# A mixture-of-experts decoder trunk on one core: VectorE's part of the overflow block's search ahead of the branch, and the down product's column halves as two tiles

## Chip, cores and metric

One core of a Trainium2 chip runs the whole program. The metric is the device time of one execution in microseconds; times are medians of several runs. Where an expert gets more tokens than its fixed slots hold, the program branches into a further block; the inputs are the same in every run.

## What is computed

Two layers on 512 tokens of 1024 columns, fp32. Each layer is a token mixer (layer 0: causal differential attention; layer 1: causal pooling over trailing windows), a layer norm, a mixture of experts, and a layer norm. The mixers are not touched by the change. The experts' part of the reference, cut down (a router picks one of 4 groups for each token and the two best of the group's 8 experts):

```python
def hier_moe(x, ..., w_gate, w_up, w_down):
    g_idx = argmax(xf @ w_grp_router + b_grp_router)            # group of a token
    top_v, top_i = top_k(expert logits in that group, 2)
    gate = g_p * softmax(top_v)
    ...                                                         # tokens sorted by expert
    def run_block(xb, e):
        h = silu(xb @ w_gate[e]) * (xb @ w_up[e])               # 1024 -> 512
        return h @ w_down[e]                                    # 512 -> 1024
    out[token] += gate * run_block(...)
h = layer_norm(alpha * h + hier_moe(h))
```

## The kernel before

All 32 experts of a layer run, two at a time (a pair, 16 pairs in a layer), each with 64 slots for tokens, so that a pair fills the 128 partitions. An expert that gets more than 64 tokens has the rest done in an overflow block behind a branch. On these inputs one overflow block runs in layer 0 and none in layer 1.

Weights come over the SyncE queue in loads of 1 MB into 21 buffers (`fill` issues as buffers come free, `take` hands them out in order). A pair takes 12 of them: 4 for gate, 4 for up, 4 for down.

`moe` (L890) holds a layer's experts. Its loop (q from 0 to 7) does an even and an odd pair:

- `gather2` (L1030, with `gather`, L905): VectorE writes a one-hot matrix G (token by slot, in `place_in`, L576 to L580, one buffer), TensorE multiplies tokens by it in four rounds of 32 matmuls (L917), and ScalarE and VectorE take each round out of PSUM to xT (L901, L903).
- `gate_of` (L1206, with `gate_up`, L961): 32 gate matmuls into psg, 32 up matmuls into psu (L969); ScalarE makes sg = silu(psg) (L976), VectorE h = sg * psu (L978).
- `flip`: four transposes of h on TensorE (L983), copied out by ScalarE (hT, L984).
- `down` (L986): 32 matmuls (L994) into y, one PSUM tile of two banks, a bank for each half of the 1024 columns. `weigh` (L1001) multiplies by the slots' weights and splits the result in a high and a low part, in a tile yy: ScalarE reads y for the high part (L1003), VectorE for the low (L1004), for each half.
- `spread_all` (L1192, with `spread_sum`, L1197): for each of four token tiles TensorE brings the yy of the two pairs before back to token rows (sc, L1201 and L1202, a PSUM tile with two buffers), and VectorE adds it to the running sum r (L1204). Column half 0 is done after an even pair's `gate_of`, half 1 after its `flip`.

The last round of the loop ends otherwise. After the odd pair's `gate_of` the engines load the number of overflow blocks and branch (L1260, L1264). Inside, SyncE fetches gate and up weights of the two experts, and `seek` (L1131) finds the block's tokens: VectorE marks the experts (hit), sums their weights (msk, wc), computes slot numbers (base, then sl, shown as msk) and what is left (rem), then writes G for the block; TensorE gathers (64 matmuls of L917), and `places` makes the way back. After the branch stand `spread_all` of half 0, `flip`, `spread_all` of half 1, and `down_spread` (L1015), which does the down product one column half after the other and puts the way back of half 0 (L1008, L1009, r in L1011) between the steps of half 1. A second branch (L1294) holds the block's gate and up product, a third (L1300) its `item_down`, again with `down_spread`. So `down_spread` runs three times: in layer 0, for the block, and in layer 1. Between the branches, `after()` of layer 0 converts the first weights of layer 1's mixer (pc: ScalarE L283, VectorE L284), and the layer ends with a norm.

TensorE's order is the order in which the program is written (`manual_schedule`, L1130). VectorE's and ScalarE's order is chosen by a scheduler, which keeps to the dependencies between tiles: a read and a write of one tile are kept in order even where they touch different halves of it.

Of the kernel before, what the change touches and what calls it, by code (L numbers as in the profile page):

```python
# [8 lines left out]
F32 = mybir.dt.float32  # L9
F32R = mybir.dt.float32r  # L10
# [54 lines left out]
def tile_trunk(ctx, tc, x, w_qkv, w_o, p_in, p_grp, p_scale, p_out,  # L65
# [180 lines left out]
    def do(steps):  # L246
        for f in steps:
            f()
# [641 lines left out]
    def moe(l, rt_in, name1, after):  # L890
        with ExitStack() as es:
# [10 lines left out]
                else:  # L902
                    V.tensor_scalar(dst, src, g, b, op0=OP.mult, op1=OP.add)  # L903

            def gather(slots, cc, xT, pairs):  # L905

                n = pairs * P
                G = keep.tile([P, NT, 2 * P], F32R, name="G", tag="G")
                for j in range(NT):
                    do(place_in(G[:, j, 0:n], slots, cc, j))  # L910

                def round(k0, ga):
                    for k in range(k0, k0 + 2):
                        for j in range(NT):
                            g = G[:, j] if pairs == 2 else G[:, j:j + 1, 0:P].to_broadcast([P, 2, P])
                            for i in range(2):
                                PE.matmul(ga[:, k - k0], half_of(xs[j], i).bitcast(F32R)[:, k], g,  # L917
                                          start=j + i == 0, stop=j + i == NT)
                    for k in range(k0, k0 + 2):
                        factor(xT[:, k, 0:n], ga[:, k - k0, 0:n], k, (ACT, V)[k % 2])  # L920

                def ga_tile(k0):
                    if k0 in (2, 4):
                        return p2.tile([P, 2, 2 * P], F32, name="ga", tag="sc")
                    return p1.tile([P, 2, 2 * P], F32, name="ga", tag="ga")

                return G, [lambda k0=k0: round(k0, ga_tile(k0)) for k0 in range(0, KD, 2)]

            def flip_places(G, i, Sm, ga):

# [55 lines left out]
            def down(hT, wd, wslot, todo=()):  # L986

                todo = list(todo)
                y = p1.tile([P, 2, 512], F32, name="y", tag="y")
                for k in range(4):  # L990
                    for c in range(2):
                        for e in range(2):
                            es_ = slice(e * CAP, (e + 1) * CAP)
                            PE.matmul(y[es_, c], hT[:, k, es_], wd(e, k, c), start=k == 0, stop=k == 3)  # L994
                    run(todo)
                yy = unit("yy")
                for c in range(2):
                    weigh(yy, y, wslot, c)
                return r32(yy)

            def weigh(yy, y, wslot, c):  # L1001
                yr = r32(yy)
                ACT.activation(yr[:, c], y[:, c], AF.Copy, scale=wslot)  # L1003
                V.scalar_tensor_tensor(yr[:, 2 + c], y[:, c], wslot, yy[:, c], op0=OP.mult, op1=OP.subtract)  # L1004

            def spread(yr, Sm, t, c, st=None):
                ps = p2.tile([P, 512], F32, name="sc", tag="sc")
# [6 lines left out]

            def down_spread(hT, wd, wslot, Sm, yy, st):  # L1015

                y = p1.tile([P, 2, 512], F32, name="y", tag="y")
                for c in range(2):
                    for k in range(4):
                        for e in range(2):  # L1020
                            es_ = slice(e * CAP, (e + 1) * CAP)
                            PE.matmul(y[es_, c], hT[:, k, es_], wd[c][e][:, k], start=k == 0, stop=k == 3)
                        if c and k < 2:
                            for t in (2 * k, 2 * k + 1):
                                spread(r32(yy), Sm, t, 0, st)
                    weigh(yy, y, wslot, c)
                for t in range(NT):
                    spread(r32(yy), Sm, t, 1, st)
# [99 lines left out]
            rt_in.region.close()  # L1128
            fill(CAP0)
            es.enter_context(tc.manual_schedule(engines={mybir.EngineType.PE}))  # L1130
            def seek(xT1, Sm1):  # L1131

                hit, left = rt([2, NE], "hit"), rt([2], "left")
                for e in range(2):
                    V.tensor_scalar(hit[:, e], cf[:, C_I32:C_I32 + NE], ixf[:, e:e + 1], None, op0=OP.is_equal)
                wc, wx = rt([2, NT], "wc"), rt([NT, 4], "wx", F32R)
                wt = wtmp
                for e in range(2):
                    V.tensor_tensor(wt, wsum, hit[:, e:e + 1].to_broadcast([P, NT, NE]), op=OP.mult)
                    V.tensor_reduce(wc[:, e], wt, axis=AX, op=OP.add)  # L1140
                split(wx[:, :, 0:2], wx[:, :, 2:4], wc[:, :, :].rearrange("p e t -> p t e"))

                base, sl = rt([2], "base"), wtmp.rearrange("p t e -> p (t e)")
                V.tensor_scalar(base, m8[:, 0:2], 0.5, 1e6, op0=OP.is_lt, op1=OP.mult)
                V.scalar_tensor_tensor(base, m8[:, 0:2], float(CAP), base, op0=OP.mult, op1=OP.add)
                V.scalar_tensor_tensor(base, ixf, float(S), base, op0=OP.mult, op1=OP.add)
                for e in range(2):
                    V.tensor_scalar(sl[:, e * CAP:(e + 1) * CAP], slotc[:, 0:CAP], base[:, e:e + 1], None, op0=OP.add)
                V.tensor_tensor(rem, rem, hit[:, 0], op=OP.subtract)
                V.tensor_tensor(rem, rem, hit[:, 1], op=OP.subtract)  # L1150
                V.tensor_scalar(rem, rem, 0.0, None, op0=OP.max)
                G1, rounds = gather(sl, code, xT1, 1)
                do(rounds)
                places(G1, wx, Sm1, ws1)

# [68 lines left out]
            for q in range(NPAIR // 2):  # L1224
                p, final = 2 * q, q == NPAIR // 2 - 1

                fill(CAPW)
                if final:
                    gb, rows_ = norm_rows(l, 1, lambda: p2.tile([P, 512], F32, name="row", tag="sc"))
                else:  # L1230
                    rows_ = [lambda i=i: residue(i) for i in (0, 2, 1, 3)]
                prev = [(yr, places_of(b)) for yr, b in prev]
                h = gate_of(p, rows_[0:2] if final else rows_[2:4] if q == 1 else ())
                if q == 0:
                    R = two("r")
                    whole(0)
                    whole(1)
                wdn = [take("d", l, p, i) for i in range(2)]
                fill(CAPW)
                if prev:  # L1240
                    spread_all(0, prev)
                else:
                    code_row(0)
                    code_row(1)
                hT = hT_tile()
                flip(h, hT)
                if prev:
                    spread_all(1, prev)
                else:
                    all_weights()  # L1250
                prev = [down_of(p, hT, wdn)]

                p += 1
                fill(5 if final else CAPW)
                h = gate_of(p, rows_[2:4] if final else rows_[0:2] if q == 0 else ())
                wdn = [take("d", l, p, i) for i in range(2)]
                if final:
                    prev = [(yr, places_of(b)) for yr, b in prev]
                    Sm, ws = places_of(p), wall[:, p:p + 1]
                    n_items = nc.values_load(items[0:1, 0:1], min_val=0, max_val=2 * MAXB)  # L1260
                    wx = [[two("wx") for _ in range(2)] for _ in range(2)]
                    xT1 = mo.tile([P, KD, 2 * P], F32, name="xT1", tag="xT")[:, :, 0:P]
                    Sm1 = mo.tile([P, S], F32R, name="Sm1", tag="Sm", bufs=3)
                    with tc.If(n_items, preferred_fallthrough_block=False):  # L1264
                        er = experts()
                        fetch(w_gate, er, wx[0])
                        fetch(w_up, er, wx[1])
                        seek(xT1, Sm1)
                    spread_all(0, prev)
                    hT = hT_tile()  # L1270
                    flip(h, hT)
                    spread_all(1, prev)
                    yy = unit("yy")
                    down_spread(hT, wdn, ws, Sm, yy, st)
                    done(4)
                else:
                    fill(CAPW)
                    xT, (G, rounds) = gather2(p + 1)
                    do(rounds[0:2])
                    hT = hT_tile()  # L1280
                    flip(h, hT)
                    do(rounds[2:4])
                    prev.append(down_of(p, hT, wdn))
# [111 lines left out]
```

## Time and profile before

| | |
|---|---|
| three runs | 1479.14, 1480.89, 1483.9 us; median 1480.89 |
| profiled execution | 1484.56 us |
| its span on the core | 1482.8 us |
| mean granted TensorE clock | 0.982 of full speed |
| busy: TensorE, VectorE, ScalarE | 96%, 44%, 23% of the span |
| DMA | 450.16 MB, mean 304 GB/s |

The span runs from the first to the last instruction; the execution's own time holds 1.76 us more. Layer 0's experts take roughly from 300 to 840 us of the span, layer 1's from 990 on. In the timeline a row gives the start and the length of one instruction or of several alike in a row, and in brackets how long the engine had been idle before it and what ended that.

### The profile page before, as it was taken

What the parts mean: (1) busy time and instruction counts of PE and PEld (TensorE: products, weight loads), DVE (VectorE), ACT (ScalarE), POOL (GpSimd) and SP (SyncE); (2) the same over time, 40 slices, a digit from 0 to 9 for tenths busy, and PEclk for the clock granted to TensorE, in tenths of its full rate; (3) what the DMA queues carried; (4) which work ended last, traced back from release to release, by engine and by line L of the source; (5) the groups of instructions that cost most, each with busy time, mean ns of one, the idle gap of its engine ahead of it and who ended that gap; (6) DMA issues with size and microseconds to landing.
All of it is one profiled execution on the core that took longest, in us unless ns stands there. A gap on an engine that the chain in (4) does not pass through costs nothing. (4 is left out here: it accounts for less than half of the span.)

```text
span 1482.8 us, 18487 instructions
## 1 busy us (share of the span) xinstructions
PE 1416.7 (96%) x7269; PEld 806.0 (54%) x7269; DVE 654.5 (44%) x1513; ACT 345.6 (23%) x714; POOL 26.9 (2%) x24
## 2 busy tenths in 40 slices
PE   8999999999999999999988699999999999999993
PEld 6766776855455445444543387864445444544541
DVE  4356358575423223313224697466423312322136
ACT  4355456421111011011111144331011011110110
POOL 0000000210000000000000000110000000000000
PEclk9999999999999999999999899999999999999997
DMA  7111505379999999999994315379999999999971
GB/s 255 59 53 33 187 13 194 128 306 392 414 417 421 421 421 421 421 421 421 421 411 164 131 57 235 115 286 389 396 422 420 422 421 420 421 421 420 422 290 58
DMA packets 85712, 450.16 MB, mean 304 GB/s; under 512 B 10664, under 2 KB 20464, under 8 KB 36464
## 3 DMA queue, kind: packets, MB, share of 16 engines
q1 hardware_dynamic: 85616, 448.86, 75.2%
q8 instruction: 62, 1.02, 0.3%
q14 instruction: 34, 0.28, 0.1%
HBM read 446.74 MB, written 2.10 MB: 303 GB/s over the span
## 5 line engine op out<-in xcount | busy, mean ns | idle before, releaser
L969 PE MATMUL psu<-w_u,xT 128*64 128x512 f32 x1024 | 225.6, 593 | 0.0
L969 PE MATMUL psg<-w_g,xT 128*64 128x512 f32 x1024 | 225.3, 593 | 0.2 <-ACT xT L901 0.2
L994 PE MATMUL y<-w_d,hT 128*64 128x512 f32 x960 | 212.6, 596 | 1.5 <-ACT hT L984 1.5
L1004 DVE SCALAR_TENSOR_TENSOR yy<-y,wall,yy 128x512 fp32r<-128x512 f32 x64 | 47.2, 738 | 330.6 <-ACT yy L1003 329.1
L969 PEld LDWEIGHTS psg<-w_g,xT 128*64 128x64 f32 x1024 | 73.4, 137 | 145.6 <-issue 141.8
L969 PEld LDWEIGHTS psu<-w_u,xT 128*64 128x64 f32 x1024 | 72.8, 137 | 142.6 <-issue 137.6
L994 PEld LDWEIGHTS y<-w_d,hT 128*64 128x64 f32 x960 | 66.3, 137 | 128.5 <-issue 123.0
L976 ACT ACTIVATE sg<-psg 128x512 f32<-128x512 f32 x33 | 19.7, 597 | 467.2 <-PE psg L969 467.1
L917 PE MATMUL ga<-G,xs 128*128 128x256 f32 x960 | 121.5, 285 | 4.3 <-DVE G L579 4.3
L917 PEld LDWEIGHTS ga<-G,xs 128*128 128x128 f32 x960 | 115.8, 191 | 16.8 <-issue 11.4
L1201 PE MATMUL sc<-yy,Sm 128*128 128x512 f32 x240 | 101.9, 424 | 6.5 <-DVE r L1204 5.2
L978 DVE TENSOR_TENSOR h<-sg,psu 128x512 f32<-128x512 f32 x33 | 35.6, 1078 | 159.2 <-PE psu L969 159.2
L1204 DVE TENSOR_TENSOR r<-r,sc 128x512 f32<-128x512 f32 x128 | 85.8, 684 | 33.4 <-PE sc L1202 33.3
L1202 PE MATMUL sc<-yy,Sm 128*128 128x512 f32 x240 | 94.8, 395 | 0.0
L291 PE MATMUL acc<-pc,xTh 128*128 128x512 f32 x192 | 77.6, 404 | 2.4 <-ACT pc L256 2.1
L292 PE MATMUL acc<-pc,xTh 128*128 128x512 f32 x192 | 77.2, 402 | 0.8 <-DVE pc L257 0.8
L293 PE MATMUL acc<-pc,xTl 128*128 128x512 f32 x192 | 77.5, 404 | 0.0
L1201 PEld LDWEIGHTS sc<-yy,Sm 128*128 128x128 f32 x240 | 45.1, 188 | 41.6 <-DVE r L1204 21.2
L901 ACT ACTIVATE xT<-ga,gcol 128x256 f32<-128x256 f32 (+1 forms) x60 | 33.5, 558 | 144.6 <-PE ga L917 144.6
L903 DVE TENSOR_SCALAR xT<-ga,gcol 128x256 f32<-128x256 f32 (+1 forms) x60 | 32.1, 534 | 68.8 <-ACT xT L901 68.8
L1003 ACT ACTIVATE yy<-y,wall 128x512 fp32r<-128x512 f32 x64 | 43.8, 684 | 59.4 <-DVE yy L1004 41.3
L984 ACT ACTIVATE hT<-tp 128x512 f32<-128x512 f32 x33 | 19.7, 598 | 147.7 <-PE tp L983 146.2
(314 smaller groups left out, 1796.3 us busy)
## 6 DMA issues: line engine op xcount, KB each, us to landing
w_g<-in_moe_w_gate_dram SPq DMA_DIRECT2D x128, 1024.0 KB
w_u<-in_moe_w_up_dram SPq DMA_DIRECT2D x128, 1024.0 KB
w_d<-in_moe_w_down_dram SPq DMA_DIRECT2D x128, 1024.0 KB
w_a<-in_attn_w_qkv_dram SPq DMA_DIRECT2D x16, 512.0 KB
x<-in_x_dram SPq DMA_DIRECT2D x8, 512.0 KB
w_v<-in_attn_w_qkv_dram SPq DMA_DIRECT2D x4, 1024.0 KB
w_wo<-in_attn_w_o_dram SPq DMA_DIRECT2D x4, 1024.0 KB
wx<-in_moe_w_gate_dram SPq DMA_DIRECT2D x4, 1024.0 KB
```

The lines of the kernel that those rows point to most:

```text
L291: PE.matmul(acc, xhl(0, k), wh, start=start and j == 0, stop=False)
L292: PE.matmul(acc, xhl(0, k), wl, start=False, stop=False)
L293: PE.matmul(acc, xhl(1, k), wh, start=False, stop=stop and j == len(order) - 1)
L917: PE.matmul(ga[:, k - k0], half_of(xs[j], i).bitcast(F32R)[:, k], g, start=j + i == 0, stop=j + i == NT)
L969: PE.matmul(ps[es_], xT[:, k, es_], ws2[e][k // 4][:, k % 4], start=k == 0, stop=k == KD - 1)
L978: V.tensor_tensor(h[:, :, :].rearrange("s k q -> s q k"), r(sg), r(gu[1]), op=OP.mult)
L994: PE.matmul(y[es_, c], hT[:, k, es_], wd(e, k, c), start=k == 0, stop=k == 3)
L1003: ACT.activation(yr[:, c], y[:, c], AF.Copy, scale=wslot)
L1004: V.scalar_tensor_tensor(yr[:, 2 + c], y[:, c], wslot, yy[:, c], op0=OP.mult, op1=OP.subtract)
L1201: PE.matmul(ps, sm, yr[:, c], start=i == 0, stop=False)
L1202: PE.matmul(ps, sm, yr[:, 2 + c], start=False, stop=i == len(ys) - 1)
L1204: V.tensor_tensor(r, r, ps, op=OP.add)
```

## The change

1. `seek` is cut in two. `aim` has VectorE's search and the writing of G for the overflow block (and the split of wc on ScalarE and VectorE); `seek` keeps the gather and the way back. In the last round `aim` is called ahead of the odd pair's `gate_of`, outside of the branch, so it runs in both layers. `gather` takes a G that is there already.
2. The PSUM tile y of two banks becomes two tiles of one bank each, y0 and y1, in `down`, `down_spread` and `weigh`.

```diff
-            def gather(slots, cc, xT, pairs):
+            def gather(slots, cc, xT, pairs, G=None):
...
-                G = keep.tile([P, NT, 2 * P], F32R, name="G", tag="G")
-                for j in range(NT):
-                    do(place_in(G[:, j, 0:n], slots, cc, j))
+                if G is None:
+                    G = slot_places(slots, cc, n)
...
+            def slot_places(slots, cc, n):
+                G = keep.tile([P, NT, 2 * P], F32R, name="G", tag="G")
+                for j in range(NT):
+                    do(place_in(G[:, j, 0:n], slots, cc, j))
+                return G
...
-                y = p1.tile([P, 2, 512], F32, name="y", tag="y")
+                y = [p1.tile([P, 512], F32, name=f"y{c}", tag=f"y{c}") for c in range(2)]
...
-                            PE.matmul(y[es_, c], hT[:, k, es_], wd(e, k, c), start=k == 0, stop=k == 3)
+                            PE.matmul(y[c][es_], hT[:, k, es_], wd(e, k, c), start=k == 0, stop=k == 3)
...
-                ACT.activation(yr[:, c], y[:, c], AF.Copy, scale=wslot)
-                V.scalar_tensor_tensor(yr[:, 2 + c], y[:, c], wslot, yy[:, c], op0=OP.mult, op1=OP.subtract)
+                ACT.activation(yr[:, c], y[c], AF.Copy, scale=wslot)
+                V.scalar_tensor_tensor(yr[:, 2 + c], y[c], wslot, yy[:, c], op0=OP.mult, op1=OP.subtract)
...
-            def seek(xT1, Sm1):
+            def aim():
 
                 hit, left = rt([2, NE], "hit"), rt([2], "left")
...
-                G1, rounds = gather(sl, code, xT1, 1)
+                return slot_places(sl, code, P), wx
+
+            def seek(xT1, Sm1, found=None):
+
+                G1, wx = found or aim()
+                G1, rounds = gather(None, None, xT1, 1, G1)
                 do(rounds)
                 places(G1, wx, Sm1, ws1)
...
+                if final:
+                    found = aim()
                 p += 1
                 fill(5 if final else CAPW)
                 h = gate_of(p, rows_[2:4] if final else rows_[0:2] if q == 0 else ())
...
-                        seek(xT1, Sm1)
+                        seek(xT1, Sm1, found)
```

The scheduler moves more than these lines show. TensorE's and SyncE's order stay as they were. VectorE's order at the branch, before (h of the last pair, then the branch and the search in it; `msk` with `base` is sl):

```order
L978 TENSOR_TENSOR h<-sg,psu 128x128x4
L1260 TENSOR_LOAD items
L1264 COMPARE_AND_BRANCH
L1264 UNCONDITIONAL_BRANCH
L1135 TENSOR_SCALAR hit<-cf,ixf 128x32 x2
L1139 TENSOR_TENSOR msk<-ph,hit 128x128
...
L1148 TENSOR_SCALAR msk<-cf,base 128x64 x2
L578 TENSOR_SCALAR G<-msk,code 128x128 x2
L579 SCALAR_TENSOR_TENSOR G<-msk,code,G 128x128 x2
```

And now:

```order
L983 TENSOR_TENSOR h<-sg,psu 128x128x4
L1272 TENSOR_LOAD items
L1276 COMPARE_AND_BRANCH
L1276 UNCONDITIONAL_BRANCH
L903 TENSOR_SCALAR xT_5635<-ga,gcol 128x128 x4
L948 COPY pwc<-pw 128x4
L952 TENSOR_TENSOR ws_3038<-pwc 64x1 x2
```

Inside the branch only the copies out of the gather and the slots' weights are left. The sixteen operations of the search stand now at the head of the layer, after `pick` and before the first h of the layer, in both layers; the eight writes of G stand among the copies (L903) of the last gather of the loop.

VectorE's order around h of an even pair in the middle of a layer, before (yy of the pair before, r of the sums):

```order
L1004 SCALAR_TENSOR_TENSOR yy_4363<-y_4346,wall_3010,yy_4363 128x512
L978 TENSOR_TENSOR h_4384<-sg_4419,psu_4402 128x128x4
L1004 SCALAR_TENSOR_TENSOR yy_4363<-y_4346,wall_3010,yy_4363 128x512
L1204 TENSOR_TENSOR r0_3101<-r0_3101,sc_4438 128x512
L1204 TENSOR_TENSOR r0_3101<-r0_3101,sc_4444 128x512
```

And now:

```order
L1009 SCALAR_TENSOR_TENSOR yy_4371<-y0_4353,wall_3010,yy_4371 128x512
L1009 SCALAR_TENSOR_TENSOR yy_4371<-y1_4354,wall_3010,yy_4371 128x512
L983 TENSOR_TENSOR h_4392<-sg_4427,psu_4410 128x128x4
L1214 TENSOR_TENSOR r0_3101<-r0_3101,sc_4446 128x512
L1214 TENSOR_TENSOR r0_3101<-r0_3101,sc_4452 128x512
```

The second yy has moved ahead of h, in all pairs but the first two and the last, where it stood there already. ScalarE's order is the same there (sg, yy, yy), but its second yy no longer waits for VectorE's first.

TensorE's order in `down_spread`, layer 0, before, at the change from half 0 to half 1 (sc: the sums of half 0; in brackets the engines and queues that a matmul waits for):

```order
L1022 MATMUL y_5790<-w_d_0_15_0_1_5427,hT_5766 64x512
L1022 MATMUL y_5790<-w_d_0_15_1_0_5556,hT_5766 64x512 [waits DMAHW3_49,DVE_49]
L1022 MATMUL y_5790<-w_d_0_15_1_1_5558,hT_5766 64x512 [waits DMAHW4_49]
L1008 MATMUL sc_5803<-yy_5789,Sm_5564 128x512 [waits Activation_49]
L1009 MATMUL sc_5803<-yy_5789,Sm_5564 128x512
```

And now:

```order
L1027 MATMUL y0_5805<-w_d_0_15_0_1_5441,hT_5781 64x512
L1027 MATMUL y1_5806<-w_d_0_15_1_0_5601,hT_5781 64x512 [waits DMAHW3_49]
L1027 MATMUL y1_5806<-w_d_0_15_1_1_5603,hT_5781 64x512 [waits DMAHW4_49]
L1013 MATMUL sc_5819<-yy_5804,Sm_5609 128x512 [waits DVE_49,Activation_49]
L1014 MATMUL sc_5819<-yy_5804,Sm_5609 128x512 [waits DVE_49]
```

The wait for VectorE has left the first matmul of half 1 and stands at the sums. At the end of layer 0 two conversions move besides: on ScalarE the half 1 yy of `down_spread` now comes ahead of one pc that it came after, and VectorE's closing norm has two pc (L284) between its steps, where it had one.

## Rows read from the trace of the kernel before

**Rows 1.** The page, busy time by engine.

```profile
PE 1416.7 (96%) x7269; PEld 806.0 (54%) x7269; DVE 654.5 (44%) x1513; ACT 345.6 (23%) x714; POOL 26.9 (2%) x24
```

**Rows 2.** Windows: length, busy time by engine, granted clock, DMA share, GB/s.

```profile
600.00:660.00 60.00, 59.70 (x308) 28.16 (x305) 17.44 (x32) 7.11 (x12) 0.00 (x0) 1.00 1.01 421
...
772.00:774.00 2.00, 2.00 (x11) 2.00 (x11) 0.00 (x0) 0.00 (x0) 0.00 (x0) 0.50 1.05 434
1434.00:1436.00 2.00, 2.00 (x12) 0.66 (x10) 0.67 (x1) 0.00 (x0) 0.00 (x0) 1.00 0.54 203
```

**Rows 3.** Timeline of SyncE, two issues of the weight queue, 24 loads apart.

```profile
631.75 1.58 SPq L147 DMA_DIRECT2D w_g<-in_moe_w_gate_dram  x2
...
690.14 0.80 SPq L147 DMA_DIRECT2D w_g<-in_moe_w_gate_dram  x2
```

**Rows 4.** TensorE's waits, whole run: us in total, times, longest.

```profile
PE sc L1201 <- DVE r L1204: 5.2, 18, 0.3
PE y L1022 <- DVE yy L1004: 4.7, 3, 1.6
```

**Rows 5.** Timeline at the branch of layer 0.

```profile
766.60 1.03 DVE L978 TENSOR_TENSOR h<-sg,psu 128x512 f32<-128x512 f32 x1 [5.09 <-PE psu L969]
767.65 0.39 DVE L1135 TENSOR_SCALAR hit<-cf,ixf 128x32 f32<-128x32 f32 x2
...
769.81 0.48 DVE L578 TENSOR_SCALAR G<-msk,code 128x128 fp32r<-128x128 f32 x2
...
770.61 0.76 PE L917 MATMUL ga<-G,xs 128*128 128x256 f32 x4 [4.08 <-DVE G L579]
...
771.61 8.82 PE L917 MATMUL ga<-G,xs 128*128 128x256 f32 x60 [0.23 <-DVE G L579]
```

**Rows 6.** Source line L1264, TensorE's branch: durations, first and last start.

```profile
L1264 PEldq COMPARE_BRANCH  x3: 75/240/307, 762.9 to 1440.1; - x3
```

**Rows 7.** Timeline, two rounds of an ordinary gather.

```profile
645.39 4.01 PE L917 MATMUL ga<-G,xs 128*128 128x256 f32 x32
```

**Rows 8.** Timeline of VectorE, the first h of layer 0.

```profile
324.57 1.04 DVE L978 TENSOR_TENSOR h<-sg,psu 128x512 f32<-128x512 f32 x1 [2.60 <-PE psu L969]
```

**Rows 9.** Timeline, the last `down_spread`, from half 0 to half 1.

```profile
1451.99 1.08 PE L1022 MATMUL y<-w_d,hT 128*64 128x512 f32 x4 [1.57 <-DVE yy L1004]
...
1453.33 0.40 PE L1009 MATMUL sc<-yy,Sm 128*128 128x512 f32 x1
```

**Rows 10.** Timeline, the first sum of half 1: layer 0, layer 1.

```profile
800.92 0.50 PE L1008 MATMUL sc<-yy,Sm 128*128 128x512 f32 x1 [1.38 <-ACT yy L1003]
...
1458.99 0.50 PE L1008 MATMUL sc<-yy,Sm 128*128 128x512 f32 x1 [0.79 <-ACTq L1294]
```

**Rows 11.** Timeline, sums of half 0 in the middle of layer 0.

```profile
674.40 1.08 DVE L978 TENSOR_TENSOR h<-sg,psu 128x512 f32<-128x512 f32 x1 [4.86 <-PE psu L969]
...
675.33 0.72 DVE L1004 SCALAR_TENSOR_TENSOR yy<-y,wall,yy 128x512 fp32r<-128x512 f32 x1
...
675.97 1.27 DVE L1204 TENSOR_TENSOR r<-r,sc 128x512 f32<-128x512 f32 x2
...
675.99 0.40 PE L1202 MATMUL sc<-yy,Sm 128*128 128x512 f32 x1
...
676.69 0.51 PE L1201 MATMUL sc<-yy,Sm 128*128 128x512 f32 x1 [0.30 <-DVE r L1204]
```

**Rows 12.** Timeline of VectorE, closing norm of layer 0.

```profile
843.41 0.70 DVE L284 SCALAR_TENSOR_TENSOR pc<-w_pin,vcol,pc 128x512 fp32r<-128x512 f32 x1
```

**Rows 13.** Timeline of TensorE, the last up product of layer 1.

```profile
1433.51 6.18 PE L969 MATMUL psu<-w_u,xT 128*64 128x512 f32 x28
```

**Rows 14.** Timeline, start of layer 1's mixer: two readers of PSUM beside TensorE.

```profile
847.56 3.86 PE L263 MATMUL pp<-cf,r 128*128 128x128 f32 x17 [8.09 <-DVE r L407]
...
849.50 1.36 DVE L257 TENSOR_TENSOR xTl<-pp,xTh 128x512 fp32r<-128x512 f32 x2
849.53 0.60 ACT L256 ACTIVATE xTh<-pp 128x512 fp32r<-128x512 f32 x1 [0.20 <-PE pp L263]
```

More of the change, by code (lines that the diff above doesn't have):

```diff
@@ L1015, in down_spread @@
             def down_spread(hT, wd, wslot, Sm, yy, st):
-                y = p1.tile([P, 2, 512], F32, name="y", tag="y")
+                y = [p1.tile([P, 512], F32, name=f"y{c}", tag=f"y{c}") for c in range(2)]
                 for c in range(2):
@@ L1021, in down_spread @@
                             es_ = slice(e * CAP, (e + 1) * CAP)
-                            PE.matmul(y[es_, c], hT[:, k, es_], wd[c][e][:, k], start=k == 0, stop=k == 3)
+                            PE.matmul(y[c][es_], hT[:, k, es_], wd[c][e][:, k], start=k == 0, stop=k == 3)
                         if c and k < 2:
```

## The prediction, made before the changed kernel was run

> **What bounds the kernel now.** I read the page first: TensorE is busy for 96% of the span [rows 1]. So the time is TensorE's own work plus its waits, and a change of VectorE's work counts only where TensorE waits for VectorE. In the middle of a layer the windows show a granted clock of 1.00 and a DMA share of 1.01 at 421 GB/s [rows 2]: TensorE runs with almost no gap, and the weight stream is as full as it gets. Two issues of the weight queue, 24 loads of 1.0486 MB apart, lie 58.39 us apart [rows 3], so TensorE takes 25.17 MB in 58.39 us, or 431 GB/s, a little more than the stream's 421. It lives off the 21 buffers that were filled ahead. Next I read TensorE's waits [rows 4], and for each group that the change touches the timeline around one of its waits.
>
> The sum is made against the profiled execution (1484.56 us), 3.67 above the median of the runs (1480.89). I take the gain as the same in both. A difference of some 4.4 us, 0.3%, is what a measurement of this kernel can tell from none.
>
> **1. The search ahead of the branch (layer 0 alone runs the block).** Before, VectorE ends h at 767.63, begins the search 0.02 us later, begins the first G at 769.81, and TensorE starts to gather at 770.61 after 4.08 us of idle time, with 0.23 more before the other 60 matmuls [rows 5]. With G written before, those 4.08 + 0.23 = 4.31 us go. TensorE's own branch stood at 762.9 [rows 6], 3.6 us before its last matmul ended (770.61 - 4.08 = 766.53), so I take the entry of the block as hidden. The gather itself took from 770.61 to 780.43, 9.82 us less 0.23 of wait, and the granted clock was 0.50 in 772 to 774 [rows 2, 5], the 1.2 GHz level of the two, after the idle time. The same 64 matmuls at full clock take two rounds of 4.01 us, 8.02 [rows 7]. In the new order TensorE comes into the gather straight from the dense up product, so I take the full clock: 1.57 us more. Together **5.9 us**. Lower bound 4.3, if the clock falls anyway. The block's fetch of expert weights stays on its queue as it is, and TensorE uses them only behind the next pair's down product and sums, so it doesn't hold the gather.
>
> What that search costs in its new place: the order puts it before the layer's first h, where VectorE was idle for 2.60 us [rows 8]. It lasted 769.81 - 767.65 = 2.16 us [rows 5]; so it fits, with 0.44 left for the small split of weights (wx) that moves along, at a price of **0**. If the cover were gone, 2.16 us in both layers would delay h, less what TensorE does there ahead of needing h (the code rows). The eight G's follow the last gather of the loop, while TensorE has a down product and a gate and up product before the next h: 0 as well. In layer 1 the search and the G's are made for nothing, at the same places.
>
> **2. Column halves in three down_spreads.** Before, the first matmul of half 1 waits until VectorE has read half 0 out of the two-bank tile: 4.7 us in 3 waits [rows 4], 1.57 in the last layer [rows 9]. In the new order that matmul waits for the weights alone. What is late next is the sum behind it: its second matmul needs VectorE's yy, which is ready at 1451.99 (TensorE's release). Four half-1 matmuls take 1.0 us and fit into the 1.57. So the second matmul of the sum moves from 1453.33 [rows 9] to 1451.99, 1.34 us earlier. Three times: **4.0 us**. The upper bound is the whole 4.7; the lower 2.8, if VectorE's read runs 0.4 later because ScalarE's next read goes beside it.
>
> **3. Half 1 in layer 0.** TensorE waited 1.38 us for ScalarE's yy, because a pc conversion stood ahead of it there; in layer 1, with nothing ahead, it was 0.79 [rows 10]. ScalarE now does yy first: **0.6 us**, between 0 and 0.6.
>
> **4. The sums in the loop.** Before, VectorE did yy, h, yy, and then the r additions; ScalarE's second yy waited for VectorE's first, and VectorE's second came after h. So r stood 0.65 us behind h (675.97 against 675.33), and TensorE, which has two PSUM buffers for the sums, waited for r [rows 11]. In the cadence of the matmuls the next would have started at 675.99 + 0.23 = 676.22; it started at 676.69: 0.47 us. Now both yy stand ahead of h (both halves of y have been finished since before the gate product), and r comes 0.65 earlier than it did, ahead of 676.22. The waits count 18 such stops, 5.2 us in all [rows 4]: one for each of the 14 even pairs that have sums between gate and flip (7 in a layer), shown as 0.30, and four in the closing pairs, where both yy stood ahead of h already. I take 0.45 for each of the 14, nearest the cadence: **6.3 us**; bounds 14 x 0.30 = 4.2 and 14 x 0.47 = 6.6.
>
> **5. What gets worse.** In layer 0's closing norm one more pc conversion of VectorE now lies between its steps. One that is there already takes 0.70 us and stands among the statistics [rows 12]. TensorE waits for the end of that chain, so the second one costs **0.7 us**; 0 at best.
>
> Sum: 5.9 + 4.0 + 0.6 + 6.3 - 0.7 = 16.1. From 1480.9 that is **1464.8 us** (1468.5 against the profiled one).
>
> **Rivals.**
> *The block's entry takes the place of the wait.* If TensorE needs until 770.6 to have the instructions of the block, 7.7 us after its branch at 762.9 [rows 6], part 1 gives nothing and the time is 1470.7. The old trace cannot exclude it, since the wait for G covers it. Against it: VectorE took the same branch and began its search 0.02 us after h [rows 5]. The Trainium skill ("Runtime: NRT & Kernel Launch", Instruction fetch mechanics) speaks for it: a taken branch to a target outside of the prefetched window makes the engine fetch by DMA before it goes on. It gives no time for that; VectorE's row shows no stall that h did not cover. Chance 0.06.
>
> *The stream becomes the bound.* At 421 GB/s [rows 2] two pairs need 25.17 / 0.421 = 59.8 us, against 58.39 of TensorE's [rows 3]; with part 4 it would be 57.9. So each two pairs eat 1.9 us of lead rather than 1.4. At the end of layer 1 the stream falls off in 1434 to 1436 [rows 2]; the last four loads are down weights, 2.5 us each at 421, so the up weights were there by about 1425. The up product's last 28 matmuls take from 1433.51 to 1439.69 [rows 13], and its second half of weights is needed from 3.7 us before that end, 1436. Some 10 us of lead are left, and part 4 takes half of its 6.3, 3.2, in a layer. If the lead were gone earlier, part 4 would be lost: 1471.1. Chance 0.07. Beside this stands the Trainium skill ("Perfetto Trace Analysis", Roofline): one core's 16 DMA engines give some 435 GB/s in all. By that estimate two pairs need 57.9 us and no lead is eaten at all; the measured 421 decides, and it leaves less room than the page does. With both of these rivals only 3.9 us are gained, 1477.0, within 0.3%: 0.04 with all cases like it.
>
> *Slower: reads of PSUM hold TensorE.* With two tiles ScalarE reads y1 while VectorE reads y0, and TensorE writes psu in the same time. If TensorE stood still for the length of such a read, the 0.72 of VectorE's yy [rows 11], in each of 30 down products of the loop, that is 21.6 us: 1486.4. It turns the gain into a loss from 16.1 / 30 = 0.54 us each. Against it: at 849.5 VectorE and ScalarE read PSUM together while TensorE transposes into it, and ScalarE's read keeps its 0.60 us [rows 14]. Chance 0.03.
>
> **How the numbers follow.** The forecast 0.80, the rivals 0.06, 0.07, 0.04 (no change), 0.03. Faster: 0.80 + 0.06 + 0.07 = 0.93. The range: all terms at their better ends give 5.9 + 4.7 + 0.6 + 6.6 - 0 = 17.8, 1463.1; at their worse ends 4.3 + 2.8 + 0 + 4.2 - 0.7 = 10.6, 1470.3, and the two faster rivals lie at 1470.7 and 1471.1. Stretches at the low clock, as at 772 [rows 2], come after TensorE's pauses, and pauses move here. By the 1.57 of part 1 I allow two of them downward and one upward: 1460 to 1472. Only the unchanged and the slower case lie outside.
>
> **What would show it.** Right: no wait for G in front of the overflow's gather, granted clock 1.00 through it, some 8.0 us for its 64 matmuls; no wait for yy ahead of half 1, and one of about 0.3 us in the sum behind it; VectorE's yy ahead of h, and the 5.2 us of waits for r [rows 4] down to about 1. Wrong: TensorE idle at the head of the block for another reason; matmuls waiting for loads late in a layer; up products with gaps; a first h that comes later than psu; or more low clock in the layers' ends.

## The result

| | us |
|---|---|
| before, median of 4 runs | 1480.64 (1479.14 to 1483.9) |
| changed, median of 4 runs | 1463.31 (1461.9 to 1464.41) |
| ratio | 0.9877, 95% interval 0.9864 to 0.989 |
| forecast | 1464.8, range 1460 to 1472 |
| profiled execution, changed | 1461.90, span 1460.1, mean granted clock 0.989 |

The change is 17.3 us faster; 16.1 were forecast. Two more sets of runs of the changed kernel gave 1463.41 and 1463.34, so it is well known. The kernel before is less well known: of its 31 timed executions beside all these runs, 15 lie from 1478.5 to 1481.6 us and 16 from 1482.3 to 1485.1, and its median depends on how many fall to each part. Beside the two later sets it was 1483.05 and 1482.49, which makes the change 19.6 and 19.2 us faster. Pieces of a few us are therefore told by runs beside the changed kernel, and by stages of the traces.

### The profile page after: what moved, and what is told of

Its sections match the earlier page's. It is cut to its first block, busy times and chain, and to the rows that moved or that the text cites. A ratio compares the mean times of both kernels' runs of the same rounds, so it can differ in the third digit from the quotient of the medians.

```text
span 1460.1 us, 18530 instructions
## 1 busy us (share of the span) xinstructions
PE 1407.3 (96%) x7269; PEld 798.7 (55%) x7269; DVE 662.2 (45%) x1536; ACT 343.1 (23%) x715; POOL 27.1 (2%) x24
## 5 line engine op out<-in xcount | busy, mean ns | idle before, releaser
L1211 PEld LDWEIGHTS sc<-yy,Sm 128*128 128x128 f32 x240 | 45.0, 187 | 36.9 <-DVE r L1214 17.1
L903 DVE TENSOR_SCALAR xT<-ga,gcol 128x256 f32<-128x256 f32 (+1 forms) x60 | 32.1, 534 | 70.8 <-ACT xT L901 70.8
L1212 PEld LDWEIGHTS sc<-yy,Sm 128*128 128x128 f32 x240 | 45.3, 189 | 6.4
```

The source lines that it names most:

```text
L1211: PE.matmul(ps, sm, yr[:, c], start=i == 0, stop=False)
L1212: PE.matmul(ps, sm, yr[:, 2 + c], start=False, stop=i == len(ys) - 1)
```

## The profile after

TensorE's busy time on the page, which answers to [rows 1]:

```profile
PE 1407.3 (96%) x7269; PEld 798.7 (55%) x7269; DVE 662.2 (45%) x1536; ACT 343.1 (23%) x715; POOL 27.1 (2%) x24
```

The instructions on TensorE are the same 7269, in 9.4 us less busy time: a part of the difference is matmuls that run at the higher clock. Against a second profile of the kernel before (the first experiment below), whose page has 1412.2 us, it is 4.9 us. VectorE has 23 instructions more, the search (fifteen; a sixteenth is ScalarE's) and the eight G of layer 1, which nobody uses.

The windows (length, busy time by engine, granted clock, DMA share, GB/s), in the middle of layer 0 and over the overflow's gather:

```profile
600.00:660.00 60.00, 60.00 (x308) 28.34 (x306) 17.82 (x32) 6.90 (x12) 0.00 (x0) 1.00 1.01 421
762.00:771.00 9.00, 8.09 (x66) 7.53 (x64) 2.70 (x5) 1.83 (x4) 0.00 (x0) 1.00 1.02 422
```

Where TensorE had 59.70 of 60 us [rows 2] it has all 60, and the granted clock stays at 1.00 through the gather, where it was 0.50 in 772 to 774. The timeline at the branch, against [rows 5]:

```profile
762.35 7.74 PE L916 MATMUL ga<-G,xs 128*128 128x256 f32 x64
762.50 1.09 DVE L983 TENSOR_TENSOR h<-sg,psu 128x512 f32<-128x512 f32 x1 [6.33 <-PE psu L974]
```

The gather begins with no idle time in front of it, before h does, and its 64 matmuls take 7.74 us. TensorE's branch stands at 758.8, as far ahead as in [rows 6]:

```profile
L1276 PEldq COMPARE_BRANCH  x3: 75/240/314, 758.8 to 1418.6; - x3
```

The sums in the loop, against [rows 11]:

```profile
665.63 1.41 DVE L1009 SCALAR_TENSOR_TENSOR yy<-y,wall,yy 128x512 fp32r<-128x512 f32 x2 [12.00 <-ACT yy L1008]
671.24 1.08 DVE L983 TENSOR_TENSOR h<-sg,psu 128x512 f32<-128x512 f32 x1 [4.20 <-PE psu L974]
672.34 0.69 DVE L1214 TENSOR_TENSOR r<-r,sc 128x512 f32<-128x512 f32 x1
...
672.60 0.40 PE L1211 MATMUL sc<-yy,Sm 128*128 128x512 f32 x1
672.84 0.40 PE L1212 MATMUL sc<-yy,Sm 128*128 128x512 f32 x1
673.08 0.50 PE L1211 MATMUL sc<-yy,Sm 128*128 128x512 f32 x1
```

Both yy are done 4.20 us before h, r follows h at once, and the fifth sum's matmuls follow at the usual 0.23 to 0.24. The last `down_spread`, against [rows 9]:

```profile
1425.33 4.51 PE L1027 MATMUL y<-w_d,hT 128*64 128x512 f32 x20
...
1429.76 0.75 DVE L1009 SCALAR_TENSOR_TENSOR yy<-y,wall,yy 128x512 fp32r<-128x512 f32 x1 [3.63 <-ACT yy L1008]
1429.78 0.49 PE L1013 MATMUL sc<-yy,Sm 128*128 128x512 f32 x1
1430.56 0.50 PE L1014 MATMUL sc<-yy,Sm 128*128 128x512 f32 x1 [0.29 <-DVE yy L1009]
```

All 16 matmuls of half 0 and the first 4 of half 1 are one row of 20, and 0.29 us of waiting are left, at the sum. TensorE's waits over the whole run, against [rows 4]:

```profile
PE pp L263 <- DVE r L407: 8.6, 1, 8.6
...
PE sc L1014 <- DVE yy L1009: 1.7, 6, 0.3
...
PE sc L1211 <- DVE r L1214: 1.0, 4, 0.3
```

The 4.7 us ahead of half 1 and the waits for G [rows 5] are gone; the waits for r went from 18 with 5.2 us to 4 with 1.0, the four of the closing pairs. Against that, the wait for layer 0's closing norm (L407) is 8.6 us, where [rows 14] show 8.09: a second pc lies in its chain.

Where the time went stage by stage, from the starts of VectorE's h in the timelines (h number 17 is the overflow's, 18 the first of layer 1). The kernel before is here a second execution (1478.88 us, the first experiment below), one of its shorter ones:

| stage | before | changed | gain | forecast |
|---|---|---|---|---|
| start of the first h | 323.45 | 323.60 | -0.15 | 0 |
| to h 16 | 441.97 | 438.90 | 3.07 | 3.15 (half of part 4) |
| to h 17 | 53.38 | 45.11 | 8.27 | 7.8 (5.9 + 1.34 + 0.6) |
| to h 18 | 173.35 | 171.84 | 1.51 | 0.6 (1.34 - 0.7) |
| to h 33 | 441.92 | 438.88 | 3.04 | 3.15 (half of part 4) |
| to the end of the span | 43.03 | 41.77 | 1.26 | 1.34 |

Together 17.0, where the forecasts of the stages make 16.1. The two halves of the loop and the end are within 0.11 us of their forecasts in this table, and two further profiles of the changed kernel (1462.05 and 1461.92 us) agree with them to 0.1. The rows to h 17 and h 18 are not so well known one by one: those profiles give gains of 9.72 and -0.30, and 9.72 and 0.05. Together the two rows gain 9.78, 9.42 and 9.77, where 8.5 were forecast. The windows show why they shift: in the first profile the clock is at 0.50 from 791 to 794, ahead of h 17, in the other two around 809 to 811, behind it.

## Experiments

**The kernel before, once more.**

> The kernel before once more, for a second profile. The first one lies 3.7 us above its median. Theory: it had a stretch at the low clock in layer 1's router that most executions don't have, and without it the ledger of the change adds up: the second profile shows no such stretch and some 1480.5. Rival: every execution has it; then the change's gain holds 3.4 us of clock that no part of the diff explains.

One execution: 1478.88 us. The windows show the same stretch of layer 1's router, in the first profile and in the second (columns as above):

```profile
976.00:983.00 7.00, 6.05 (x33) 5.79 (x32) 2.51 (x7) 0.16 (x1) 1.01 (x1) 0.54 0.74 265
```

```profile
971.00:978.00 7.00, 4.78 (x40) 4.23 (x38) 4.40 (x11) 1.89 (x4) 2.65 (x2) 1.00 0.95 366
```

The granted clock was 0.54 there in the first and 1.00 in the second. From h 16 to h 18 the first took 4.5 us longer, 3.25 of them between the first transposes behind layer 0's closing norm (L263) and h 18, where the router lies. So most of the 5.7 us between the two spans goes with the clock, and it is there or not in one and the same kernel. That most executions are without it, as was expected, doesn't follow: about half of the 31 lie with the first profile. Whether the router makes the difference in all of these isn't shown, as only two were traced.

In the second profile the low clock lay on the whole head of the overflow's gather instead:

```profile
769.42 10.15 PE L917 MATMUL ga<-G,xs 128*128 128x256 f32 x64 [4.08 <-DVE G L579]
```

**The two tiles alone.**

```diff
-                if final:
-                    found = aim()
...
-                        seek(xT1, Sm1, found)
+                        seek(xT1, Sm1)
```

> The change without its first part: the search stays in the branch, y is two tiles. If the parts add up, the 5.9 us of the branch come back on top of 1463.3: about 1469.2, and the trace shows 4.1 us of TensorE waiting for G and a low clock in the overflow's gather, with no wait for yy ahead of half 1 and no wait for r in the loop. Rival, that the parts overlap because the layer's end takes its pace from something else than TensorE (the weight stream, the norm): nearer to 1463 to 1465.

1468.08 us (1467.64 to 1469.79), ratio to before 0.9908 (0.9892 to 0.9925). TensorE's waits:

```profile
PE ga L916 <- DVE G L579: 4.3, 2, 4.1
```

and nothing ahead of half 1 or for r in the loop. Against the changed kernel 4.8 us are lost by the medians, where 5.9 were expected: the wait is back in full and the gather takes 9.6 us of work again (0.76 and 8.85 in its two rows). Between the traced executions 5.9 to 6.1 are lost (spans of 1466.2 against 1460.1, 1460.3 and 1460.2), so the traces bear out the 5.9; why the medians have 1.1 less is open. The rival, 1463 to 1465, is out.

**The search alone.** y is one tile of two banks again (the diff's lines on y undone).

> The change without its second part: the search ahead of the branch, y one tile of two banks. Theory: 5.9 us less than before, about 1474.7; the waits for r (5.2 us, 18 times) and for yy (4.7 us, 3 times) are there as before. Rival, that the search is not covered at the head of the layers: its 2.16 us come in twice and leave 1.6, about 1479.0.

1473.38 us (1472.67 to 1475.41), ratio 0.9942 (0.9929 to 0.9955). TensorE's waits are those of before:

```profile
PE sc L1211 <- DVE r L1214: 5.2, 18, 0.3
PE y L1027 <- DVE yy L1009: 4.7, 3, 1.6
```

So none of the loop's gain comes from the search. Against the changed kernel this is 10.1 us slower by the medians, and 10.2 were forecast for the two tiles (4.0 + 0.6 + 6.3 - 0.7). The spans of the traced executions differ by 11.9 to 12.1, so the close agreement is in part luck. The rival, an uncovered search, is out, and the changed kernel's own timeline shows the cover, against [rows 8]:

```profile
323.60 1.04 DVE L983 TENSOR_TENSOR h<-sg,psu 128x512 f32<-128x512 f32 x1 [0.50 <-PE psu L974]
```

Of the 2.60 us of idle time 0.50 are left: the search took 2.10 of it, and h still waits for TensorE.

Beside the kernel before in their own set (median 1481.62), the parts alone gained 8.2 and 13.5, 21.8 in all, more than the whole change. Against the changed kernel they are worth 4.8 and 10.1, 14.8 in all. So by the medians alone it can't be told whether the parts add up.

The changed kernel was run again beside the kernel before with this question. If the parts are as forecast, with 0.5 for the closing norm, it should be 16.3 us faster; if each part brings the 1 to 2 us more that it showed alone, 18 to 21. The medians were 1463.41 and 1483.05, 19.6 apart, which speaks for the second. But the nine executions of the kernel before in that set reach from 1478.5 to 1485.1, and the span of this profile is 16.8 us below that of the second profile before (1460.3 against 1477.1). The medians don't decide it; the stages above put 0.9 to 1.3 us more than forecast between h 16 and h 18, and nothing more elsewhere.

**The second yy behind h again, with two tiles.**

```diff
-                for c in range(2):
-                    weigh(yy, y, wslot, c)
+                weigh(yy, y, wslot, 0)
+                late.append(lambda: weigh(yy, y, wslot, 1))
...
# at the end of the next gate_of
+                do(late)
+                late.clear()
```

> All of the change, but the weighing of column half 1 is written after the next pair's h, so that VectorE has yy, h, yy again while y stays in two tiles. Theory, that the 6.3 us of the loop come from the place of VectorE's second yy ahead of h: they are lost, about 1469.6, with 14 or more waits for r. Rival, that they come from the two tiles as such (ScalarE no longer waits for VectorE's read): no change, 1463.3.

1468.88 us (1466.32 to 1471.69): 5.6 slower than the change. The timeline of VectorE has the old order back, and the waits the old sum:

```profile
674.43 1.09 DVE L983 TENSOR_TENSOR h<-sg,psu 128x512 f32<-128x512 f32 x1 [4.86 <-PE psu L974]
675.37 0.71 DVE L1011 SCALAR_TENSOR_TENSOR yy<-y,wall,yy 128x512 fp32r<-128x512 f32 x1
```

```profile
PE sc L1213 <- DVE r L1216: 5.3, 18, 0.3
```

The starts of h show it most plainly: from h 1 to h 16 this kernel takes 442.10 us, where the two profiles of before have 442.03 and 441.97 and the change 438.90; in layer 1 it is the same (442.11, 441.96 and 441.92, 438.88), so 6.4 us come back in the loop. ScalarE does its two yy one after the other here, as with the change. What gains in the loop is thus VectorE's order, and not the tiles as such.

Whether two tiles are needed for that order isn't shown. In the kernel before ScalarE's second yy was done well ahead of h at 674.40 [rows 11]:

```profile
669.57 0.69 ACT L1003 ACTIVATE yy<-y,wall 128x512 fp32r<-128x512 f32 x1 [0.82 <-DVE yy L1004]
```

VectorE then sat idle until h, so its second yy of 0.72 us would have fitted there with one tile as well. The scheduler put it behind h. One tile with that order written by hand was not run.

**The first sum ahead of half 1.**

```diff
                 for c in range(2):
+                    if c:
+                        spread(r32(yy), Sm, 0, 0, st)
                     for k in range(4):
...
-                            for t in (2 * k, 2 * k + 1):
+                            for t in ((1,), (2, 3))[k]:
```

> All of the change, but in down_spread the first sum of half 0 stands ahead of half 1's matmuls, so that TensorE waits for VectorE's yy where it waited before. Theory, 1.34 us in each of three places: 4.0 us lost, about 1467.3, with three waits of some 1.5 us ahead of the sum. Rival, that the time saved there is waited for later anyway (at r, or in the norm): no change, 1463.3.

1465.64 us (1465.0 to 1466.7): 2.3 slower, not 4.0. The timeline of the last `down_spread`:

```profile
1431.57 0.50 PE L1013 MATMUL sc<-yy,Sm 128*128 128x512 f32 x1 [0.79 <-ACT yy L1008]
1432.36 0.50 PE L1014 MATMUL sc<-yy,Sm 128*128 128x512 f32 x1 [0.28 <-DVE yy L1009]
1432.78 1.08 PE L1029 MATMUL y<-w_d,hT 128*64 128x512 f32 x4
```

TensorE waits for ScalarE's yy and then again for VectorE's, with half 1 behind both. From h 33 to the end of the span it takes 42.97 us (1420.13 to 1463.1), where the changed kernel takes 41.77: 1.20 lost in this `down_spread`, 3.6 in three. The scheduler moved pc as well, in both directions. In layer 0 one stands ahead of ScalarE's yy of half 1 again, so the 0.6 of part 3 is lost too:

```profile
790.29 0.50 PE L1013 MATMUL sc<-yy,Sm 128*128 128x512 f32 x1 [1.38 <-ACT yy L1008]
```

And both pc are out of VectorE's closing norm, where TensorE's wait fell by 1.0 us, from 8.6 to 7.6. 3.6 + 0.6 - 1.0 = 3.2, against 2.8 to 3.0 between the traced executions and 2.3 between the medians.

This prices part 5. VectorE's chain in that norm, from the start of L401 to the start of L407, holds one pc before, two with the change and none in this run (one pair of rows each):

```profile
843.06 0.43 DVE L401 BATCH_NORM_AGGREGATE lnmva<-bnst 128x2 f32<-128x12 f32 x4 [0.81 <-DVEq L1303]
...
846.60 2.98 DVE L407 TENSOR_SCALAR r<-r,rs_yla,lnnm 128x1024 f32<-128x1024 f32 x4
```

```profile
828.24 0.43 DVE L401 BATCH_NORM_AGGREGATE lnmva<-bnst 128x2 f32<-128x12 f32 x4 [0.81 <-DVEq L1315]
...
832.30 2.98 DVE L407 TENSOR_SCALAR r<-r,rs_yla,lnnm 128x1024 f32<-128x1024 f32 x4
```

```profile
831.30 0.42 DVE L401 BATCH_NORM_AGGREGATE lnmva<-bnst 128x2 f32<-128x12 f32 x4 [0.81 <-DVEq L1317]
...
834.35 2.98 DVE L407 TENSOR_SCALAR r<-r,rs_yla,lnnm 128x1024 f32<-128x1024 f32 x4
```

It takes 3.54, 4.06 and 3.05 us: 0.5 for each pc, though the instruction itself lasts 0.70.

**Only the search ahead, G in the block.**

```diff
-                return slot_places(sl, code, P), wx
+                return sl, wx
...
-                G1, wx = found or aim()
-                G1, rounds = gather(None, None, xT1, 1, G1)
+                sl, wx = found or aim()
+                G1, rounds = gather(sl, code, xT1, 1)
```

> All of the change, but only the search stands ahead of the branch: the eight writes of G stay in the block. TensorE then waits some 2.0 us for the first G and 0.2 more, where it waited 4.1 before and 0 with the change. Theory, that the low clock in the gather came from the length of the wait and a wait of 2 us does not bring it: 2.2 us slower than with the change, clock 1.00 in the gather, 64 matmuls in 8. Rival, that any wait there brings it: 3.8 us slower, and a stretch at 0.5.

1465.65 us: 2.2 slower than the changed kernel beside it (1463.41). The median agrees with the theory, but the five runs lie at 1465.2, 1465.3, 1465.7 and at 1467.0, 1467.4, and the profile is of the run at 1467.0, in which the clock did fall. Timeline and windows:

```profile
765.50 0.77 PE L916 MATMUL ga<-G,xs 128*128 128x256 f32 x4 [1.90 <-DVE G L579]
...
766.41 8.78 PE L916 MATMUL ga<-G,xs 128*128 128x256 f32 x60 [0.15 <-DVE G L579]
```

```profile
766.00:768.00 2.00, 1.85 (x9) 1.64 (x9) 0.62 (x3) 0.00 (x0) 0.00 (x0) 0.59 1.03 430
768.00:770.00 2.00, 2.00 (x12) 2.00 (x11) 0.12 (x1) 0.46 (x1) 0.00 (x0) 0.56 0.99 414
```

So here a wait of 1.90 us was followed by the low clock and 9.5 us of gather instead of 7.7; from h 16 to h 18 this execution takes 3.6 to 4.0 us more than the three profiles of the changed kernel, as the rival has it. The three faster runs would fit a gather without the low clock, but none of them was traced, and the mean granted clock doesn't tell the runs apart (0.989 at 1467.41 and at 1465.19). Neither side of the expectation holds alone.

Over all twelve profiles the gather goes with its wait: in the eight in which it starts without one, the granted clock is 1.00 from 760 to 780; in the four in which it waits (twice before, the tiles alone, and here) it falls there.

**TensorE kept busy in the closing norm, 52 matmuls.** The computation stays whole; the added results are not used.

```diff
+            warm(acc_tile(), 52)
             for t in range(NT):
                 transpose_hl(R, *xT, t, lambda c: pp_tile())
```

> All of the change, and 52 matmuls of 128x256 on constants, whose result nobody reads, in the 8.6 us in which TensorE waits for layer 0's closing norm. Theory, that the low clock of about 10 us at the start of layer 1's mixer comes from that idle time and costs TensorE up to half of the 5 us in which it works there: 1.5 to 2.9 us faster than the change. Rival, that the transposes there are paced by the copies of VectorE and ScalarE: the clock is 1.00 and the time is the same within 0.5.

1464.77 us (1462.38 to 1465.6) against 1463.41 (1462.05 to 1463.94) beside it: no gain. The added matmuls came late:

```profile
829.38 7.50 PE L310 MATMUL acc<-cb 128*128 128x256 bf16 x52 [3.84 <-DVE lnmva L401]
```

They waited 3.84 us for the norm's first step (the PSUM bank comes free with it) and the norm's transposes began behind them at 836.72, where the three profiles of the changed kernel begin them at 833.26, 833.09 and 833.45.

**The same with 26 matmuls, and the changed kernel beside it.**

> All of the change, and 26 instead of 52 matmuls on constants in TensorE's wait for layer 0's closing norm. With 52 they began 4 us later than meant, since their PSUM bank comes free only when the norm has begun, and ended 2.6 us after the norm was ready, which took back what the clock gave. Theory: 26 end with the norm, the transposes start in time at clock 1.00, 1.3 to 2.4 us faster than the change beside it. Rival, that the copies of VectorE and ScalarE pace that stage: within 0.5 of the change.

> The changed kernel, to stand beside the run with 26 matmuls on one chip: 1463.4 as in its earlier runs, or the two chips differ by more than the 1 to 2 us in question.

1461.42 us (1461.27 to 1462.73) against 1463.34 (1461.92 to 1464.33): by the medians 1.9 faster, in the middle of what was expected, with four runs each and ranges that overlap. Their ratios to before are 0.9867 (0.9847 to 0.9886) and 0.9879 (0.9859 to 0.9898). Timeline and window of the run with 26:

```profile
828.75 4.63 PE L310 MATMUL acc<-cb 128*128 128x256 bf16 x26 [4.08 <-DVE lnmva L401]
...
833.28 1.94 PE L263 MATMUL pp<-cf,r 128*128 128x128 f32 x16
```

```profile
832.00:834.00 2.00, 2.00 (x19) 1.69 (x18) 1.93 (x5) 0.00 (x0) 0.00 (x0) 0.97 0.00 0
```

The transposes begin in time and at the full clock, 16 of them in 1.94 us, where the changed kernel took 5.35 for 24, with the granted clock at 0.50 from 830 to 838.

The traces bear out the clock, but not the whole size. From the first transpose to h 18 this run takes 145.47 us and the three profiles of the changed kernel 146.19, 146.47 and 145.97; from h 16 to h 18 the gain is 0.7 to 1.0, and the spans differ by 0.6 to 0.8 (1459.5 against 1460.1 to 1460.3). So 0.5 to 1.0 us is what the traces show, and the rest of the 1.9 may be chance. The rival holds in part: behind these 16 transposes TensorE waits 0.25 us for ScalarE's copy, the next ones start at 835.96, and of TensorE's waits one later in the mixer grows (L846 on ScalarE's pT, 1.2 us, where L845 of the changed kernel has 0.5).

## Why the prediction was right

The three mechanisms that carry the sum (the wait for G, the wait of half 1, VectorE's order in the loop) each lost their gain when they were taken back. The size is right as well, though 16.1 against 17.3 holds some luck, told at the end of this section.

1. **The branch**, forecast 5.9: right, slightly small. The 4.08 (and 0.23) of waiting went whole, so the entry of the block was hidden behind the up product, and the first rival falls: the gather starts with no idle time. The Trainium skill's statement on taken branches ("Runtime: NRT & Kernel Launch", Instruction fetch mechanics) may hold, but its price doesn't show here, with TensorE's branch 3.6 us ahead of the gather. The clock's part was 1.85 us against the first profile (9.59 of work to 7.74) and 2.41 against the second, not 1.57: the gather at full clock takes 7.74, less than the 8.02 of two rounds of an ordinary one.
2. **`down_spread`**, 4.0: right. The wait of 1.57 became 0.29 at the sum, 1.28 each; the last stage of the table has 1.26. When the wait was put back, 1.20 were lost there.
3. **Half 1 in layer 0**, 0.6: right. The row that answers to the first of [rows 10] waits 0.79 for ScalarE, as in layer 1:

```profile
788.73 0.49 PE L1013 MATMUL sc<-yy,Sm 128*128 128x512 f32 x1 [0.79 <-ACT yy L1008]
```

4. **The loop**, 6.3: right, and the best known: 3.07 and 3.04, steps of 0.42 to 0.47 at each of the 14 even pairs. VectorE's order makes it, as the run with the late half shows.
5. **The closing norm**, -0.7: the sign was right, the size is 0.5 by VectorE's chain.

The search's new place cost nothing, as forecast. The weight stream did not become the bound: TensorE's waits name no DMA in either layer's loop, and the loop's steps keep their 0.45 to the last pair. Nor did two readers of PSUM hold TensorE: the up matmuls take 593 ns each before and after, and VectorE's yy went from 738 to 747 ns.

What the sum didn't hold is that the executions of the kernel before lie several us apart. The sum was made against one of the longer ones and taken off the median of three runs, two of which were of the shorter ones. The spans differ by 22.7 us against the first profile and by 17.0 against the second; the medians by 17.3, and by 19.6 and 19.2 in the later sets, where the forecast said 16.1. That the first set came so near is luck in part: its kernel before was mostly of the shorter kind. Against the second profile the sum is about 1 us short, all of it between h 16 and h 18. The gather's clock (2.41 for 1.57) and the closing norm (0.5 for 0.7) answer for that; which other stretch is at the low clock there moves from one execution to the next.

## What to carry to other kernels

One PSUM tile with two halves ties engines together that use different halves, and the costliest tie may be an order that the scheduler then chooses on one of them, even where another would have fitted: compare the whole order, and look at what stands in front of the instruction that the bound engine waits for. Work that only the branch needs, but that is known much earlier, belongs in an idle gap of its engine ahead of the branch; the gap is read from the idle time in front of a row, and afterwards the rest of it shows how much was left. A wait of the matmul engine can cost more than its length: behind the 4.08 us in front of the gather the low clock took 1.85 to 2.41 us more, and it was gone in every profile without the wait. A wait that can't be removed may be worth filling, if the filler ends in time; here that gained 0.5 to 1.0 us in the traces. And a ledger of a few us needs more than one profile of each kernel.

## What was not expected

The granted clock moves several us about in one kernel. The kernel before had 0.54 in layer 1's router in one profile and 1.00 in the other. None of the ten profiles of the changed kernel and its variants had low clock there, and three sets of runs of the changed kernel lie within 1461.9 to 1464.4. Why they stay clear of it is open: the router lies some 130 us behind the last place that the change touches. A wait of only 1.90 us was followed by a clock of 0.56 to 0.59. And in the changed kernel's first profile the clock fell to 0.50 at 791, behind waits of 0.79, 0.29 and 0.32 us, where the two others had 1.00 and fell near 809 instead, behind 1.33 and 0.75.
